# Attention on one core: value matmuls dealt out one by one between score pairs, in step with ScalarE's tiles

## The chip, the cores and the metric

The kernel runs on one core of a Trainium2 chip. The metric is the device time of one execution in microseconds (us).

## The reference

Multi-query attention: 8 batches, 1024 positions, 16 heads of 64, and one key and one value head for each batch.

```python
q = q.transpose(0, 2, 1, 3)
k = k[:, None, :, :]
v = v[:, None, :, :]
scores = np.matmul(q, k.transpose(0, 1, 3, 2)) / np.sqrt(head_dim)
weights = np.exp(scores - np.max(scores, axis=-1, keepdims=True))
weights = weights / np.sum(weights, axis=-1, keepdims=True)
attn_out = np.matmul(weights, v)
return attn_out.transpose(0, 2, 1, 3)
```

Inputs and output are float32. The kernel computes in float16 with float32 sums and leaves out the maximum; a flag at the end sends unfit inputs to a general path, which does not run here.

## The kernel before

The work is cut into 1024 **steps**. Step u makes one **tile**: the scores of 128 keys against 512 queries of two heads (128 x 1024). A pair of heads has two chunks of 512 queries, and a chunk has eight key tiles (`NKT = 8`), so eight steps in a row make one set.

- `scores` (L241): two matmuls (L247), one for each head, into a PSUM tile `sc`. The pool has three such buffers, used in turn, so tile u can be written when tile u-3 has been read.
- Each tile is turned into weights by one engine. Every fifth step from 8 to 1005 (`to_vector`, `VE_EVERY = 5`) goes to VectorE: `vector_exp` reads `sc` once (L211), and four more operations (L217, L227, L235, L237) make three float16 planes `we` out of it. They wait in a list, `pend`, of which `step` takes two for each step. All other tiles go to ScalarE: one ACTIVATE (L260) into `wt`.
- `values` (L307): the products with the values come in **groups**: 128 queries of one head, over the eight tiles of a set, one matmul for a ScalarE tile and three for a VectorE tile (L318). Sets have one or two VectorE tiles, so a group has 10 or 12 matmuls. A set has eight groups, numbered like the steps. Seven groups share one PSUM bank `ot` of two; when a bank is full it is put into `late`, and `inverse` (L263) and `finish` (L272) on VectorE divide by the sums (the 65th column) and store.
- TensorE, VectorE and ScalarE run their instructions in the order in which this program gives them (`manual_schedule`). The main loop takes two steps at a time (`BATCH = 2`): both score tiles, the operations out of `pend`, then value groups that lie `LAG = 18` steps back, then loads of what comes later (`after`):

```python
for _ in range(2 * BATCH):
    if u0 < HURRY:
        ready = nxt < u0 + BATCH - LAG
    else:
        ready = nxt < STEPS - GRP and nxt // GRP * NKT + NKT + 4 <= u0
    if ready:
        pa, ra = divmod(nxt, PSTEPS)
        values(pa, *divmod(ra, NKT))
        nxt += 1
```

So two whole groups (20 or 24 matmuls) follow each pair of score tiles, and from step `HURRY = 1012` on up to four. `last_values` (L331) makes the last set's eight groups tile by tile into two banks `otl` (L344) behind the loop.

Of the kernel before, what the change touches and what calls it, by code (L numbers as in the profile page):

```python
# [28 lines left out]
def attention_main(ctx, tc, q, k, v, out, flag):  # L29
# [14 lines left out]
    NKT = S // P  # L44
    QCH = 512
    NCH = S // QCH
    HP = H // 2
    NP = B * HP
    NQB = QCH // P
    GRP = 2 * NQB  # L50
    NG = NP * NCH * GRP
    GB = 7
# [25 lines left out]
    kv = {}  # L78
    q16 = {}
    qt = {}  # L80
    wt = {}
    osb = {}
    ot = {}
    pend = []
    product = []
    late = []
# [48 lines left out]
    def bank(name):  # L135
        return op.tile([P, 512], FP32, tag="ot", name=name)
# [104 lines left out]
    def scores(p, c, j, by_vector):  # L241
        b = p // HP
        sc = scp.tile([P, 2, QCH], FP32, tag="sc", name=f"sc{p}_{c}_{j}")
        k2t = kv[b]["k2t"]
        for hh in range(2):
            r = 64 * hh
            nc.tensor.matmul(  # L247
                sc[:, hh, :],
                k2t[r : r + 64, j * P : (j + 1) * P],
                qt[b][r : r + 64, p % HP, c * QCH : (c + 1) * QCH],  # L250
                start=True,
                stop=True,
                tile_position=(r, 0),
            )
        if by_vector:
            vector_exp(sc, p, c, j)
            return
        w = wtp.tile([P, 2, QCH], FP16, tag="wt", name=f"wt{p}_{c}_{j}")
        wt[(p, c, j)] = [(w, 0)]
        nc.scalar.activation(out=w, in_=sc, func=EXP, scale=escale, bias=math.log(CS))  # L260

    def inverse(o, g0, n):
        nc.vector.reciprocal(out=rec_all[:, g0 : g0 + n], in_=o[:, 0:n, D])  # L263

    def finish(o, g0, n):

        rec = rec_all[:, g0 : g0 + n]
        i0 = g0 % (OCH * GRP)
        if i0 == 0:
            osb[0] = osbp.tile([P, OCH * GRP, D], FP32, tag="osb", name=f"osb{g0}")  # L270
        ob = osb[0]
        nc.vector.tensor_tensor(  # L272
            out=ob[:, i0 : i0 + n, :],
            in0=o[:, 0:n, 0:D],
            in1=rec.unsqueeze(2).broadcast_to([P, n, D]),
            op=ALU.mult,
        )
        while stored[0] < g0 + n:
            e = stored[0]
            e += GRP // 2 if e >= NG - GRP else GRP  # L280
            if e > g0 + n:
                break
            store(ob, stored[0], e)
            stored[0] = e
        per = HP * NCH * GRP
        if g0 + n == NG:
            check(g0 - GRP // 2, NG, ok_all[:, B:])
        elif checked[0] < B and g0 + n >= min((checked[0] + 1) * per, NG - GRP):
            e = min((checked[0] + 1) * per, NG - GRP)
            b = checked[0]  # L290
            check(b * per, e, None, ok_all[:, b : b + 1])
            checked[0] += 1

    def store(ob, g0, g1):
        p, c = divmod(g0 // GRP, NCH)
        b, hp = divmod(p, HP)
        q0 = c * QCH + g0 % GRP // 2 * P
        j0 = g0 % (OCH * GRP)
        n = g1 - g0
        nc.sync.dma_start(  # L300
            out=out[b, q0 : q0 + n // 2 * P, 2 * hp : 2 * hp + 2, :].rearrange(
                "(qb p) h d -> p qb (h d)", p=P
            ),
            in_=ob[:, j0 : j0 + n, :].rearrange("p (qb h) d -> p qb (h d)", h=2),
        )

    def values(p, c, g):  # L307

        b = p // HP
        qb, hh = divmod(g, 2)  # L310
        gg = (p * NCH + c) * GRP + g
        if gg % GB == 0:
            ot[0] = bank(f"ot{gg}")[:, 0 : GB * 72].rearrange("p (g f) -> p g f", f=72)
        o = ot[0]
        vp = kv[b]["vp"]
        terms = [(j, w, i) for j in range(NKT) for w, i in wt[(p, c, j)]]
        for n, (j, w, i) in enumerate(terms):
            nc.tensor.matmul(  # L318
                o[:, gg % GB, 0 : D + 1],
                w[:, hh, qb * P : (qb + 1) * P],  # L320
                vp[:, i, j, 0 : D + 1],
                start=(n == 0),
                stop=(n == len(terms) - 1),
            )
        if gg % GB == GB - 1 or gg == NG - GRP - 1:
            late.append((o, gg - gg % GB, gg % GB + 1))
        if g == GRP - 1:
            for j in range(NKT):
                del wt[(p, c, j)]

    def last_values():  # L331

# [23 lines left out]
    def check(g0, g1, each, all_=None):  # L356
        n = g1 - g0
        rec = rec_all[:, g0:g1]
        ge = chkp.tile([P, n], FP32, tag=f"ge{n}", name=f"ge{g0}")
        nc.vector.tensor_scalar(  # L360
            out=ge, in0=rec, scalar1=1.0 / SUM_HI, scalar2=None, op0=ALU.is_ge
        )
        both = each
        if both is None:
            both = chkp.tile([P, n], FP32, tag=f"both{n}", name=f"both{g0}")
        nc.vector.scalar_tensor_tensor(  # L366
            out=both, in0=rec, scalar=1.0 / SUM_LO, in1=ge, op0=ALU.is_le, op1=ALU.mult
        )
        if all_ is not None:
            nc.vector.tensor_reduce(out=all_, in_=both, axis=AX.X, op=ALU.min)  # L370

    LAG = 2 * NKT + 2
    STEPS = NP * NCH * NKT
    PSTEPS = NCH * NKT
    BATCH = 2
    LAST_VE = (STEPS - 2 * NKT) // VE_EVERY * VE_EVERY
    HURRY = STEPS - NKT - 4

    def to_vector(u):
        return u % VE_EVERY == 0 and NKT <= u <= LAST_VE  # L380

    def step(u):
        p, r = divmod(u, PSTEPS)
        c, j = divmod(r, NKT)
        scores(p, c, j, to_vector(u))
        for _ in range(2):
            if pend:
                pend.pop(0)()
        if product and u >= LAST_VE + 2 and not pend:
            product.pop()()  # L390

    def after(u):
        p, r = divmod(u, PSTEPS)
# [24 lines left out]
    with tc.manual_schedule():  # L418
        load_kv(0)
        load_q_first(0)  # L420
        make_identity(nc, ident)
        for p in range(1, NFIRST):
            load_q_first(p)
        load_v(0)
        for c in range(NKT):
            load_q(0, c)
        for t in vps:
            for i, ci in enumerate((1.0, C0, C3)):
                nc.gpsimd.memset(t[:, i, :, D : D + 1], ci)
        nc.vector.tensor_copy(out=ident16, in_=ident)  # L430
        nc.vector.memset(ones, 1.0)
        kps = bank("kps0").bitcast(FP16)
        turned[0] = bank("qps0").bitcast(FP16)
        lo, hi = range(NKT // 2), range(NKT // 2, NKT)
        q0 = q16[("first", 0)]
        nc.scalar.copy(out=q0[:, 0 : NKT // 2, :], in_=qf[:, 0 : NKT // 2, :])  # L436
        first_k(kps, 0)
        first_q(turned[0], 0, lo)
        first_q_out(turned[0], 0, lo, nc.scalar.copy)
        first_k_out(kps, 0)  # L440
        first_k(kps, 1)
        first_k_out(kps, 1)
        nc.vector.tensor_copy(out=q0[:, NKT // 2 :, :], in_=qf[:, NKT // 2 :, :])
        prep_v(0)
        for c in range(NKT):
            turn_q(0, c)
        nxt = 0
        for u0 in range(0, STEPS, BATCH):
            us = range(u0, u0 + BATCH)
            for u in us:  # L450
                step(u)
            for f in late:
                pend.insert(0, lambda f=f: inverse(*f))
                pend.insert(min(2, len(pend)), lambda f=f: finish(*f))
            del late[:]
            for _ in range(2 * BATCH):
                if u0 < HURRY:
                    ready = nxt < u0 + BATCH - LAG
                else:
                    ready = nxt < STEPS - GRP and nxt // GRP * NKT + NKT + 4 <= u0  # L460
                if ready:
                    pa, ra = divmod(nxt, PSTEPS)
                    values(pa, *divmod(ra, NKT))
                    nxt += 1
            for u in us:
                after(u)
        assert nxt == STEPS - GRP
        assert not product
        for f in pend:
            f()  # L470
        for f in late:
            inverse(*f)
            finish(*f)
        last_values()
        okm = chkp.tile([P, 1], FP32, tag="okm", name="okm")
        nc.vector.tensor_reduce(out=okm, in_=ok_all, axis=AX.X, op=ALU.min)
        cnt = bank("cnt")[0:1, 0:1]
        nc.tensor.matmul(cnt, okm, ones, start=True, stop=True)
        nc.vector.tensor_scalar(
            out=flag, in0=cnt, scalar1=P - 0.5, scalar2=None, op0=ALU.is_lt  # L480
        )
# [120 lines left out]
```

## Time and profile before

| | |
|---|---|
| median of 3 runs | 782.24 us (781.58 to 783.35) |
| profiled execution | 783.46 us, span 781.5 us |
| ScalarE (ACT) busy | 98% |
| TensorE (PE) busy | 93% |
| VectorE (DVE) busy | 93% |
| GpSimd (POOL) busy | 8% |

A line of the profile names the engine, the line of the kernel (L260), the operation, output<-input, how often, the busy time, and the idle time before it with the engine that ended it. In the timeline the columns are the start in us, the length in us, engine, line, operation and count, and in brackets how long the engine had been idle and what it waited for. In the table by windows, each engine's busy time is followed by its count in brackets, then the granted TensorE clock, the DMA share and GB/s. PE is the matmuls, PEld the weight loads; the matmul lengths overlap.

### The profile page before, as it was taken

What the parts mean: (1) busy time and instruction counts of PE and PEld (TensorE: products, weight loads), DVE (VectorE), ACT (ScalarE), POOL (GpSimd) and SP (SyncE); (2) the same over time, 40 slices, a digit from 0 to 9 for tenths busy, and PEclk for the clock granted to TensorE, in tenths of its full rate; (3) what the DMA queues carried; (4) which work ended last, traced back from release to release, by engine and by line L of the source; (5) the groups of instructions that cost most, each with busy time, mean ns of one, the idle gap of its engine ahead of it and who ended that gap; (6) DMA issues with size and microseconds to landing.
All of it is one profiled execution on the core that took longest, in us unless ns stands there. A gap on an engine that the chain in (4) does not pass through costs nothing.

```text
span 781.5 us, 30669 instructions
## 1 busy us (share of the span) xinstructions
PE 728.7 (93%) x13474; PEld 474.1 (61%) x13474; DVE 728.9 (93%) x1349; ACT 762.5 (98%) x827; POOL 65.9 (8%) x99
## 2 busy tenths in 40 slices
PE   5999999999999999999999999999999999999996
PEld 2566666656666666666656666666666666666665
DVE  3899999999999999999999999999999999999992
ACT  7999999999999999999999999999999999999996
POOL 4210002100011002010020100201002100000000
PEclk8899999999999999999999999999999999999999
DMA  9949118582193813756155552556417373111113
GB/s 169 146 93 164 55 44 157 97 136 57 29 170 76 154 33 76 150 103 115 45 91 123 124 95 56 90 128 115 101 42 125 89 149 71 51 35 55 43 43 84
DMA packets 168633, 73.84 MB, mean 94 GB/s; under 512 B 93744, under 2 KB 161328, under 8 KB 168496
## 3 DMA queue, kind: packets, MB, share of 16 engines
q1 hardware_dynamic: 148864, 53.76, 32.5%
q0 software_dynamic: 18576, 17.57, 14.8%
q8 instruction: 106, 1.74, 1.0%
q10 hardware_dynamic: 1056, 0.52, 0.3%
q14 instruction: 31, 0.25, 0.1%
HBM read 37.75 MB, written 33.55 MB: 91 GB/s over the span
## 4 chain that ended last, share of the span: by engine, by line
ACT 38%; DVE 21%; PE 21%; issue 19%; DMA 1%; DVEq 0%; ACTq 0%
ACT wt L260 38%; PE ot L318 11%; PE sc L247 9%; DVE we L211 8%; DVE osb L272 3%; DVE we L237 3%; DVE mm L235 3%; DVE m L217 2%; DVE we L227 2%; DVE rec_all L263 1%; DMA qf<-in_q_dram 1%; PE otl L344 0%; DVE both L366 0%; DVE ok_all L370 0%; DVE ge L360 0%
## 5 line engine op out<-in xcount | busy, mean ns | idle before, releaser
L260 ACT ACTIVATE wt<-sc 128x1024 f16<-128x1024 f32 x824 | 760.0, 1062 | 7.4 <-PE sc L247 6.1
L318 PE MATMUL ot<-vp,wt 128*128 128x65 f16 x6528 | 418.4, 194 | 0.6 <-issue 0.6
L318 PEld LDWEIGHTS <-wt 128*128 128x128 f16 x6528 | 325.8, 98 | 114.8 <-issue 114.8
L247 PE MATMUL sc<-qt,k2t 64*128 64x512 f16 x2048 | 352.8, 386 | 41.2 <-ACT wt L260 29.1
L318 PE MATMUL ot<-vp,we 128*128 128x65 f16 x4800 | 352.2, 193 | 0.0
L318 PEld LDWEIGHTS <-we 128*128 128x128 f16 x4800 | 250.0, 97 | 30.6 <-issue 30.6
L211 DVE TENSOR_SCALAR we<-sc 128x1024 int16<-128x1024 f32 x200 | 243.6, 1218 | 23.2 <-PE sc L247 22.1
L247 PEld LDWEIGHTS <-k2t 64*128 64x128 f16 x2048 | 93.2, 94 | 149.0 <-issue 111.0
L237 DVE TENSOR_TENSOR we<-we,mm 128x1024 f16<-128x1024 f16 x200 | 136.9, 685 | 0.0
L235 DVE TENSOR_TENSOR mm<-m 128x1024 f16<-128x1024 f16 x200 | 136.5, 683 | 0.0
L272 DVE TENSOR_TENSOR osb<-ot,rec_all 128x448 f32<-128x448 f32 x146 | 90.5, 620 | 4.2 <-DVE rec_all L263 0.2
L217 DVE TENSOR_SCALAR m<-we 128x1024 int16<-128x1024 int16 x200 | 85.8, 429 | 0.0
L227 DVE TENSOR_SCALAR we<-we 128x1024 int16<-128x1024 int16 x200 | 83.5, 418 | 0.0
L104 POOL DMA_DIRECT2D vp<-in_v_dram x8 | 7.5, 936 | 388.5 <-PE ot L318 388.4
L121 POOL DMA_DIRECT2D q<-in_q_dram x64 | 35.0, 571 | 26.7 <-DMA qt<-q 22.9
L263 DVE RECIPROCAL rec_all<-ot 128x7 f32<-128x7 f32 x146 | 28.6, 196 | 8.7 <-PE ot L318 8.6
L190 POOL TENSOR_SCALAR k16d<-knat 128x512 f16<-128x512 f32 x14 | 21.4, 1537 | 134.7 <-DMA knat<-in_k_dram 134.7
L202 DVE TENSOR_SCALAR vp<-vp 128x512 f16<-128x512 f16 x16 | 3.9, 286 | 2.0 <-DMA vp<-in_v_dram 2.0
L155 PE MATMUL kps<-ident,k 128*64 128x128 f16 x16 | 1.3, 314 | 4.5 <-DVE k L146 4.5
L184 DVE COPY qt<-qps 128x512 f16<-128x512 f16 (+1 forms) x2 | 1.1, 554 | 3.3 <-PE qps L171 3.3
L155 PEld LDWEIGHTS <-k 128*64 128x64 f16 x16 | 0.8, 159 | 4.7 <-DVE k L146 4.7
L436 ACT ACT_TABLE_LOAD x1 | 1.3, 1283 | 1.9 <-issue 1.9
(29 smaller groups left out, 22.2 us busy)
## 6 DMA issues: line engine op xcount, KB each, us to landing
out_dram<-osb SPq DMA_DIRECT2D x127, 256.0 KB, 2.4
q<-in_q_dram POOLq DMA_DIRECT2D x56, 256.0 KB, 8.8
knat<-in_k_dram SPq DMA_DIRECT2D x7, 256.0 KB, 4.1
q<-in_q_dram POOLq DMA_DIRECT2D x8, 192.0 KB, 8.0
vp<-in_v_dram POOLq DMA_DIRECT2D x8, 128.0 KB, 4.4
qt<-q SPq DMA_TRANSPOSE x64, 3.9
qf<-in_q_dram ACTq DMA_DIRECT2D x2, 256.0 KB, 4.4
knat<-in_k_dram SPq DMA_DIRECT2D x2, 128.0 KB, 3.8
```

The source lines that it names most:

```text
L121: nc.gpsimd.dma_start(out=q16[(b, c)], in_=q[b, c * P : (c + 1) * P, h0:, :].rearrange("p h d -> p (h d)"),)
L190: nc.gpsimd.tensor_scalar(out=k16d[:, :, i, :], in0=st["knat"], scalar1=kscale, scalar2=None, op0=ALU.mult)
L211: nc.vector.tensor_scalar(out=t, in0=sc, scalar1=15.0 * 1024, scalar2=0.0, op0=ALU.add, op1=ALU.max)
L217: lambda: nc.vector.tensor_scalar(out=m.bitcast(I16), in0=t, scalar1=0x3FF, scalar2=0x3C00, op0=ALU.bitwise_and, op1=ALU.bitwise_or,)
L227: lambda: nc.vector.tensor_scalar(out=w3[:, 0].bitcast(I16), in0=t, scalar1=0x7C00, scalar2=None, op0=ALU.bitwise_and,)
L235: pend.append(lambda: nc.vector.tensor_tensor(out=m2, in0=m, in1=m, op=ALU.mult))
L237: lambda: nc.vector.tensor_tensor(out=w3[:, 2], in0=w3[:, 1], in1=m2, op=ALU.mult)
L247: nc.tensor.matmul(sc[:, hh, :], k2t[r : r + 64, j * P : (j + 1) * P], qt[b][r : r + 64, p % HP, c * QCH : (c + 1) * QCH], start=True, sto ...
L260: nc.scalar.activation(out=w, in_=sc, func=EXP, scale=escale, bias=math.log(CS))
L263: nc.vector.reciprocal(out=rec_all[:, g0 : g0 + n], in_=o[:, 0:n, D])
L272: nc.vector.tensor_tensor(out=ob[:, i0 : i0 + n, :], in0=o[:, 0:n, 0:D], in1=rec.unsqueeze(2).broadcast_to([P, n, D]), op=ALU.mult,)
L318: nc.tensor.matmul(o[:, gg % GB, 0 : D + 1], w[:, hh, qb * P : (qb + 1) * P], vp[:, i, j, 0 : D + 1], start=(n == 0), stop=(n == len(terms ...
```

## The change

The value matmuls are no longer given out in whole groups. `values` now returns a list of single matmuls, and `plan` works out in advance how many of them shall have been given out by the end of each pair of steps. It reckons that a tile of ScalarE stands for a constant number of matmul times (`each`), that the two score tiles of a pair use up `OTHER = 21` of them, and it pulls the sum by an eighth of the difference towards the number that lies one group ahead of the former order. Values may lie up to two groups further ahead than before (`AHEAD = 2`). From step 1010 on (`HURRY`, before 1012) whole groups follow again, up to four for each pair of steps, and a set's groups may come two steps earlier than before. When a bank is full, the operations `inverse` and `finish` are put at the head of `pend` with one other operation between them; when two are full at once, they follow each other.

```diff
-    def values(p, c, g):
-        b = p // HP
+    def values(gg):
+        p, c = divmod(gg // GRP, NCH)
+        g = gg % GRP
...
         terms = [(j, w, i) for j in range(NKT) for w, i in wt[(p, c, j)]]
-        for n, (j, w, i) in enumerate(terms):
+
+        def one(n, j, w, i):
+            last = n == len(terms) - 1
             nc.tensor.matmul(
                 o[:, gg % GB, 0 : D + 1],
                 w[:, hh, qb * P : (qb + 1) * P],
                 vp[:, i, j, 0 : D + 1],
                 start=(n == 0),
-                stop=(n == len(terms) - 1),
+                stop=last,
             )
...
+        return [lambda n=n, t=t: one(n, *t) for n, t in enumerate(terms)]
...
+    OTHER = 21
+    AHEAD = 2
-    HURRY = STEPS - NKT - 4
+    HURRY = STEPS - NKT - 6
...
+    def plan():
+        at = range(LAG, HURRY, BATCH)
+        tiles = [sum(not to_vector(u) for u in range(u0, u0 + BATCH)) for u0 in at]
+        upto = [0]
+        for g in range(HURRY - LAG + AHEAD):
+            many = sum(to_vector(g // GRP * NKT + j) for j in range(NKT))
+            upto.append(upto[-1] + NKT + 2 * many)
+        each = (upto[HURRY - LAG] + OTHER * len(tiles)) / sum(tiles)
+        due, done = {}, 0.0
+        for u0, n in zip(at, tiles):
+            done += each * n - OTHER
+            done += (upto[u0 + BATCH - LAG + 1] - done) / 8
+            due[u0] = round(done)
+        return due
...
-        nxt = 0
+        nxt = made = 0
+        todo = []
+        due = plan()
         for u0 in range(0, STEPS, BATCH):
             us = range(u0, u0 + BATCH)
             for u in us:
                 step(u)
+            new = []
             for f in late:
-                pend.insert(0, lambda f=f: inverse(*f))
-                pend.insert(min(2, len(pend)), lambda f=f: finish(*f))
+                new += [lambda f=f: inverse(*f), lambda f=f: finish(*f)]
+            if len(new) == 2:
+                new[1:1] = pend[:1]
+                del pend[:1]
+            pend[:0] = new
             del late[:]
-            for _ in range(2 * BATCH):
-                if u0 < HURRY:
-                    ready = nxt < u0 + BATCH - LAG
-                else:
-                    ready = nxt < STEPS - GRP and nxt // GRP * NKT + NKT + 4 <= u0
-                if ready:
-                    pa, ra = divmod(nxt, PSTEPS)
-                    values(pa, *divmod(ra, NKT))
-                    nxt += 1
+            if u0 < HURRY:
+                while made < due.get(u0, 0):
+                    if not todo:
+                        if nxt >= u0 + BATCH + AHEAD - LAG:
+                            break
+                        todo = values(nxt)
+                        nxt += 1
+                    todo.pop(0)()
+                    made += 1
+            else:
+                for _ in range(2 * BATCH):
+                    if not todo and nxt < STEPS - GRP and nxt // GRP * NKT + NKT + 2 <= u0:
+                        todo = values(nxt)
+                        nxt += 1
+                    for f in todo:
+                        f()
+                    todo = []
             for u in us:
                 after(u)
```

More of the change, by code (lines that the diff above doesn't have):

```diff
@@ L305, in store @@
         )
-    def values(p, c, g):
-        b = p // HP
+    def values(gg):
+        p, c = divmod(gg // GRP, NCH)
+        g = gg % GRP
         qb, hh = divmod(g, 2)
-        gg = (p * NCH + c) * GRP + g
         if gg % GB == 0:
@@ L314, in values @@
         o = ot[0]
-        vp = kv[b]["vp"]
+        vp = kv[p // HP]["vp"]
         terms = [(j, w, i) for j in range(NKT) for w, i in wt[(p, c, j)]]
-        for n, (j, w, i) in enumerate(terms):
+        def one(n, j, w, i):
+            last = n == len(terms) - 1
             nc.tensor.matmul(
@@ L322, in values @@
                 start=(n == 0),
-                stop=(n == len(terms) - 1),
+                stop=last,
             )
[L325 to L329, printed above, removed]
+            if not last:
+                return
+            if gg % GB == GB - 1 or gg == NG - GRP - 1:
+                late.append((o, gg - gg % GB, gg % GB + 1))
+            if g == GRP - 1:
+                for x in range(NKT):
+                    del wt[(p, c, x)]
+        return [lambda n=n, t=t: one(n, *t) for n, t in enumerate(terms)]
     def last_values():
```

## The prediction

> **What bounds the kernel now.** I read the page's engine shares and chain first, then the waits over the whole span, then the timeline of single tiles. A tile is one 128x1024 block of scores (two matmuls of L247); I number tiles 0 to 1023 in their order, and name places by the last digit, because every tenth pair of steps has the same mix: digits 0 and 5 go to VectorE (L211, "V0", "V5"), the other eight to ScalarE (L260, "A1" to "A9"). S4 is the score of tile 4.
>
> ```profile
> span 781.5 us, 30669 instructions
> PE 728.7 (93%) x13474; PEld 474.1 (61%) x13474; DVE 728.9 (93%) x1349; ACT 762.5 (98%) x827; POOL 65.9 (8%) x99
> PEclk8899999999999999999999999999999999999999
> ACT 38%; DVE 21%; PE 21%; issue 19%; DMA 1%; DVEq 0%; ACTq 0%
> L260 ACT ACTIVATE wt<-sc 128x1024 f16<-128x1024 f32 x824 | 760.0, 1062 | 7.4 <-PE sc L247 6.1
> ...
> PE sc L247 <- ACT wt L260: 29.1, 96, 0.5
> DVE we L211 <- PE sc L247: 22.1, 45, 1.3
> PE sc L247 <- DVE we L211: 7.6, 19, 0.9
> ACT wt L260 <- PE sc L247: 6.1, 19, 0.7
> ```
>
> ScalarE is 98% busy, but the chain runs through three engines, so they wait on each other. The granted clock is full but for the first slices, so a stretch of matmuls keeps its length. The waits (total, times, longest) say how: TensorE's scores stand still for a buffer that ScalarE still reads, 96 times, about once for each ten tiles, while ScalarE waits visibly only 19 times. There are three score buffers, so S7 can't be written before A4 is done. That wait sits at one place:
>
> ```profile
> 436.49 1.09 ACT L260 ACTIVATE wt<-sc 128x1024 f16<-128x1024 f32 x1
> 437.39 1.11 ACT L260 ACTIVATE wt<-sc 128x1024 f16<-128x1024 f32 x1
> 437.63 0.39 PE L247 MATMUL sc<-qt,k2t 64*128 64x512 f16 x2 [0.37 <-ACT wt L260]
> 438.29 1.12 ACT L260 ACTIVATE wt<-sc 128x1024 f16<-128x1024 f32 x1
> 438.69 0.39 PE L247 MATMUL sc<-qt,k2t 64*128 64x512 f16 x2
> 439.20 1.13 ACT L260 ACTIVATE wt<-sc 128x1024 f16<-128x1024 f32 x1
> ...
> 437.62:438.68 1.06, 0.72 (x20) 0.67 (x20) 1.00 0.53 147
> ```
>
> These are tiles 574 to 578. A574 starts at 436.49, ends at 437.58, S577 starts at 437.63 (1.14 after A574's start), then 20 value matmuls (the row by window, x20), then S578 at 438.69, and A578 at 439.20, which is 0.51 behind its score. ScalarE's pace is 0.90 a tile (436.49, 437.39, 438.29, 439.20), and the least distance from a score's start to its activation is 0.49 (next rows), so with 20 values this place has 0.02 us to spare.
>
> ```profile
> 411.17 1.22 DVE L211 TENSOR_SCALAR we<-sc 128x1024 int16<-128x1024 f32 x1
> 412.44 0.39 PE L247 MATMUL sc<-qt,k2t 64*128 64x512 f16 x2 [0.83 <-DVE we L211]
> 413.61 0.39 PE L247 MATMUL sc<-qt,k2t 64*128 64x512 f16 x2
> 413.83 0.38 PE L247 MATMUL sc<-qt,k2t 64*128 64x512 f16 x2
> 414.10 1.02 ACT L260 ACTIVATE wt<-sc 128x1024 f16<-128x1024 f32 x1
> 415.48 1.02 ACT L260 ACTIVATE wt<-sc 128x1024 f16<-128x1024 f32 x1 [0.36 <-PE sc L247]
> ...
> 412.44:413.60 1.16, 0.84 (x24) 0.79 (x24) 1.00 1.16 217
> ...
> 440.07 0.39 PE L247 MATMUL sc<-qt,k2t 64*128 64x512 f16 x2
> 440.50 1.22 DVE L211 TENSOR_SCALAR we<-sc 128x1024 int16<-128x1024 f32 x1 [0.35 <-PE sc L247]
> ```
>
> Here are the other links: V540 starts at 411.17 and S543, which takes its buffer, at 412.44 (1.27). S543 to S544 takes 1.17 with 24 values between; S544 to S545 0.22; S544 to A544 0.49; S580 to V580 0.43. The row at 415.48 is A546, a digit 6: it comes 1.38 behind A544 instead of 0.90, since 24 values stood between S545 and S546. That is the loss the change goes for: after a pair with a V tile ScalarE has one tile less to live on.
>
> **The change part by part.** Instruction counts of all engines and queues stay as they are; the value matmuls are only dealt out differently between the score pairs, and their LDWEIGHTS with them. The plan's arithmetic: 11088 value matmuls over 496 pairs and 794 ScalarE tiles give (11088 + 21 x 496) / 794 = 27.08 a tile, so a pair with two ScalarE tiles is followed by 2 x 27.08 - 21 = 33, one with a V tile by 6, moved by an eighth of the lead. Over ten steps that comes out as 7 to 9 behind pair (0,1), 32 or 33 behind (2,3), 7 or 8 behind (4,5), 33 or 34 behind (6,7) and 29 to 32 behind (8,9); before, each had 20 or 24.
>
> What a longer stretch costs is in the trace, near the end:
>
> ```profile
> 769.28 0.60 PE L247 MATMUL sc<-qt,k2t 64*128 64x512 f16 x4
> 769.81 1.19 PE L318 MATMUL ot<-vp,wt 128*128 128x65 f16 x32
> 770.93 0.75 PE L247 MATMUL sc<-qt,k2t 64*128 64x512 f16 x4
> ...
> 769.50:770.92 1.42, 1.11 (x32) 1.06 (x32) 1.00 0.00 0
> ```
>
> 32 values make 1.65 from pair to pair, 1.43 from the second score on; one value is (1.06 - 0.10)/31 = 0.031 of weight loading. From the 24-value row the second score to the next pair is 1.17 + 0.031 x (n - 24): 1.46 for 33.3, 1.39 for 31, 1.43 for 32.5.
>
> Now the path that sets the end. S7 still waits for A4, whatever stood before it: three buffers, in turn. From A4's start: S7 +1.14, S8 +1.46, so S8 is at 2.60 and A8 could start at 3.09. But between A4 and A8 ScalarE has only A6 and A7 (5 is VectorE's): it is ready at 3 x 0.90 = 2.71. A8 is 0.38 late, where now it is on time. The lateness is handed on: S9 +0.22, S10 behind 31 values +1.39, V10 +0.43 (VectorE idle, as at 440.50), S13 into V10's buffer +1.27, S14 behind 32.5 values +1.43, A14 +0.49. A4 to A14:
>
> 1.14 + 1.46 + 0.22 + 1.39 + 0.43 + 1.27 + 1.43 + 0.49 = 7.83 us for ten tiles.
>
> Each step is a fixed precedence (buffer, TensorE's order, data), so ten tiles can't be faster than that. Now they take two L211 intervals:
>
> ```profile
> L211 DVE TENSOR_SCALAR we<-sc 128x1024 int16<-128x1024 f32 x183 | 222.9, 1218 | 17.6 <-PE sc L247 16.5
> ```
>
> 183 of them lie in the window from 60 to 740 us, 680/183 x 2 = 7.43. The same loop with 22.4 values in each stretch (1.12 each) is 6.91, below 7.43, so it doesn't bind today. The difference is +0.40 us, times 99 tens from step 18 to 1008: +39.6. The gain at digits 2 and 6 (S2 and S6 come behind 7 or 8 values) is inside that comparison: there TensorE will stand waiting for A9's and A3's buffers instead. Bounds for the loop: a value by the 20 and 24 rows alone, (1.17 - 1.06)/4 = 0.0275, gives 1.43, 1.36 and 1.40, sum 7.74; the 32-value row with 0.031 on it gives 1.47, 1.40, 1.45, sum 7.87. I take the middle row, which is nearest in kind (stretches with we tiles).
>
> VectorE: 728.9 us busy over 102 tens is 7.1 each, hidden under 7.83 with 0.7 to spare. The changed order in pend only matters when two inverse and finish pairs come together, which 34 values (four group ends at most, where a bank closes at every seventh) can't make: nothing. Values run up to two groups ahead: a first value then needs tile u0-8 at step u0; the product of a V tile is issued at u0-3, whose buffer S(u0) itself waits for: nothing, at most 0.1 a ten if it shows. Output stores (SP) and loads (POOL) keep their steps: nothing, by the chain's 1% DMA.
>
> The end:
>
> ```profile
> 7.35 17.55 ACT L260 ACTIVATE wt<-sc 128x1024 f16<-128x1024 f32 x19 [0.70 <-PE sc L247]
> ...
> 767.32 6.67 ACT L260 ACTIVATE wt<-sc 128x1024 f16<-128x1024 f32 x7
> 772.96 0.62 DVE L272 TENSOR_TENSOR osb<-ot,rec_all 128x448 f32<-128x448 f32 x1 [0.17 <-DVE rec_all L263]
> 773.64 2.33 PE L344 MATMUL otl<-vp,wt 128*128 128x65 f16 x64 [0.84 <-DVE osb L272]
> 775.89 0.18 DVE L263 RECIPROCAL rec_all<-otl 128x4 f32<-128x4 f32 x1 [1.21 <-PE otl L344]
> ```
>
> ScalarE ends at 773.99, but L344 starts at 773.64 because the finish at 772.96 frees its bank, and its end releases 775.89. Hurrying two steps earlier puts the last 32 values behind pair 1020 and none behind 1022: the finish moves up by about 1.6 (770.93 against 769.28), L344 is then left with the eight matmuls of the last tile after 773.99, 0.4 with their latency: -1.5. If the bank still comes late, 0. The 40 to 48 values that two groups a step bring stand behind pairs whose four tiles are all ScalarE's: 1.14 + 1.17 + 24 x 0.031 + 0.49 = 3.54 against 4 x 0.90: nothing.
>
> Sum: +39.6 - 1.5 = +38 on the profiled execution's 783.46; on the median of the runs, 782.24 (the profiled one is 1.2 above it), 820.
>
> **Weighed against the skill.** ScalarE's 0.90 enters the 2.71. The Trainium skill, ScalarE: Activation LUTs, section What ACT_TABLE_LOAD costs, gives 186 ns + 0.833 N with immediate operands and an overlap of 93, an estimate of 0.946 a tile here. By it eight tiles would need 7.57, more than the 7.43 measured, so the trace disagrees and decides; the loop of 7.83 would be the same by both, as it only passes A4 and A14, and the first rival's 7.59 would be 7.82.
>
> **The rivals.**
> One: only ScalarE's leg counts. If the V10 leg were shorter than its rows (A14 not delayed again), A8's lateness alone remains: 1.14 + 1.46 + 0.49 + 5 x 0.90 = 7.59, +0.16 a ten, +15.8 - 1.5: 797. For it: VectorE often starts late now for its own queue's sake. Against it: each of its links is a row above. Chance 0.12.
>
> Two: worse. VectorE's inverse and finish or a check fall in front of V10 and join the loop; +0.2 a ten would be about 0.6 for a third of the tens, +20: 840. Against it: the 0.7 to spare. Chance 0.06.
>
> Three, the other side: S8 is not held. ScalarE's visible waits close and nothing takes their place: -6.1 and -1.5 of the end, 775 (all of ScalarE's distance to its pace, the 766.6 from 7.35 to 773.99 less 824 x 0.90 = 742, would be 25, and 757). It decides at 21 values behind (6,7): up to there S8 starts by 2.71 - 0.49 = 2.22 after A4; 33 are dealt. It could hold if S7's release came 0.38 earlier than in the row at 437.63. Chance 0.07. The Trainium skill's Perfetto Trace Analysis, section Optimization Strategy, says to take the most-contended engine, find its gaps and make what ends them start sooner; by that rule, which looks at the 98% engine alone, this rival would be the forecast, and the 96 waits for a buffer are what it leaves out.
>
> Four: gain at 2 and 6 and loss at 8 cancel, 782. Against it: the loop is a sum, not a balance. Chance 0.03.
>
> **How the numbers follow.** My forecast has 0.72, with 808 to 832 as its own range (7.71 to 7.95 a ten: the loop's bounds of 7.74 and 7.87, with 0.03 less and 0.08 more for the length of an activation, which the rows show at 1.02 to 1.13). With rival one the range is 796 to 832 and leaves out 0.16. A measurement of this kernel tells about 0.2% (1.6 us) from no change: slower 0.90 (forecast and rivals one and two), same 0.03, faster 0.07.
>
> **What would show it.** In the changed kernel: L211 every 3.9 us in the mean instead of 3.7; S7's wait for ScalarE longer than now, and S8 starting directly behind some 33 values, with ScalarE idle about 0.25 in front of A8 and a little in front of A14; ScalarE's visible wait for scores from 6.1 to over 20 us in total; visible waits at digits 2 and 6 gone; VectorE waiting for S0. L344 ending within 0.5 of ScalarE's end. I am wrong if S8 starts within 2.22 of A4, if V10 doesn't start 0.43 behind S10, or if TensorE is found at a value matmul ahead of a waiting score.

## The result, and the profile after

The changed kernel takes 821.29 us (median of five runs, 820.98 to 821.70) against 782.24: ratio 1.0497, 95% interval 1.0483 to 1.0512. It is 39 us slower; the forecast was 820.

The page and the waits of the changed kernel (total us, times, longest us):

```profile
span 819.2 us, 30668 instructions
PE 727.7 (89%) x13474; PEld 461.0 (56%) x13474; DVE 731.1 (89%) x1349; ACT 779.3 (95%) x827; POOL 66.9 (8%) x99
L260 ACT ACTIVATE wt<-sc 128x1024 f16<-128x1024 f32 x824 | 776.8, 1029 | 29.8 <-PE sc L247 21.8
...
DVE we L211 <- PE sc L247: 59.9, 93, 2.3
PE sc L247 <- DVE we L211: 43.2, 98, 0.9
PE sc L247 <- ACT wt L260: 32.8, 106, 0.5
ACT wt L260 <- PE sc L247: 21.8, 96, 1.3
PE ot L321 <- DVE osb L272: 4.3, 10, 1.3
```

Every engine does the same work with less of its time: TensorE went from 93% to 89%, VectorE from 93% to 89%, ScalarE from 98% to 95%. No engine became the bound; they wait for each other in turn. TensorE waits for VectorE's buffer 98 times (19 before) and ScalarE for scores 96 times (19 before): about once for each ten tiles, as a closed path of ten tiles would have it.

One turn of it in the timeline (start, length, engine, operation, idle time before it and its releaser):

```profile
434.65 0.61 PE L247 MATMUL sc<-qt,k2t 64*128 64x512 f16 x4
435.15 1.02 ACT L260 ACTIVATE wt<-sc 128x1024 f16<-128x1024 f32 x1 [0.39 <-PE sc L247]
435.51 0.39 PE L247 MATMUL sc<-qt,k2t 64*128 64x512 f16 x2
436.22 0.39 PE L247 MATMUL sc<-qt,k2t 64*128 64x512 f16 x2 [0.32 <-ACT wt L260]
437.69 0.61 PE L247 MATMUL sc<-qt,k2t 64*128 64x512 f16 x4
438.18 5.80 ACT L260 ACTIVATE wt<-sc 128x1024 f16<-128x1024 f32 x6 [0.18 <-PE sc L247]
439.31 0.61 PE L247 MATMUL sc<-qt,k2t 64*128 64x512 f16 x4
439.75 1.23 DVE L211 TENSOR_SCALAR we<-sc 128x1024 int16<-128x1024 f32 x1 [0.74 <-PE sc L247]
440.20 0.39 PE L247 MATMUL sc<-qt,k2t 64*128 64x512 f16 x2
441.02 0.39 PE L247 MATMUL sc<-qt,k2t 64*128 64x512 f16 x2 [0.43 <-DVE we L211]
442.47 0.60 PE L247 MATMUL sc<-qt,k2t 64*128 64x512 f16 x4
...
436.50:437.69 1.19, 1.15 (x34) 1.09 (x34) 1.00 1.07 229
```

Read it from S4 (434.65): A4 at 435.15 (ScalarE had been idle 0.39); S7 at 436.22, when A4's buffer is free (1.07); then 34 values (the row by window) and S8 at 437.69 (1.47); A8 at 438.18, idle before it, 3.03 behind A4 where its pace would give 2.71; pair (0,1) at 439.31 (1.62 from pair to pair); V10 at 439.75, VectorE idle 0.74 before it; S13 at 441.02, released by V10 (1.27); S14 at 442.47 (1.45). S4 to S14 is 7.82. Over the whole span, by the first and last L211 of each kernel, before and after (count; shortest, median and longest in ns; first and last start):

```profile
L211 DVE TENSOR_SCALAR we<-sc x200: 1209/1216/1225, 15.5 to 756.7; 128x1024 int16<-128x1024 f32 x100
...
L211 DVE TENSOR_SCALAR we<-sc x200: 1209/1224/1225, 15.4 to 796.0; 128x1024 int16<-128x1024 f32 x100
```

(796.0 - 15.4)/199 x 2 = 7.84 us for ten tiles; before, 7.45. That is +0.39 in each of 99 tens. The end got shorter:

```profile
810.29 2.90 ACT L260 ACTIVATE wt<-sc 128x1024 f16<-128x1024 f32 x3
...
811.23 2.43 PE L351 MATMUL otl<-vp,wt 128*128 128x65 f16 x64 [0.30 <-DVE osb L272]
```

ScalarE ends at 813.19, the span at 819.2: 6.0, against 7.5 before (773.99 and 781.5).

### The profile page after: what moved, and what is told of

Its sections match the earlier page's. It is cut to its first block, busy times and chain, and to the rows that moved or that the text cites. A ratio compares the mean times of both kernels' runs of the same rounds, so it can differ in the third digit from the quotient of the medians.

```text
span 819.2 us, 30668 instructions
## 1 busy us (share of the span) xinstructions
PE 727.7 (89%) x13474; PEld 461.0 (56%) x13474; DVE 731.1 (89%) x1349; ACT 779.3 (95%) x827; POOL 66.9 (8%) x99
## 3 DMA queue, kind: packets, MB, share of 16 engines
q8 instruction: 106, 1.74, 0.9%
## 4 chain that ended last, share of the span: by engine, by line
PE 35%; ACT 34%; DVE 17%; issue 12%; DMA 1%; ACTq 0%; DVEq 0%; SPq 0%
ACT wt L260 34%; PE ot L321 21%; PE sc L247 13%; DVE we L211 8%; DVE osb L272 2%; DVE we L237 2%; DVE mm L235 2%; DVE m L217 1%; DVE we L227 1%; DVE rec_all L263 0%; DMA qf<-in_q_dram 0%; DMA knat<-in_k_dram 0%; PE otl L351 0%; ACTq L260 0%; DVE vp L202 0%
## 5 line engine op out<-in xcount | busy, mean ns | idle before, releaser
L260 ACT ACTIVATE wt<-sc 128x1024 f16<-128x1024 f32 x824 | 776.8, 1029 | 29.8 <-PE sc L247 21.8
L247 PE MATMUL sc<-qt,k2t 64*128 64x512 f16 x2048 | 349.2, 386 | 76.7 <-DVE we L211 43.2
L321 PE MATMUL ot<-vp,we 128*128 128x65 f16 x4800 | 358.1, 193 | 0.3 <-DVE osb L272 0.3
L211 DVE TENSOR_SCALAR we<-sc 128x1024 int16<-128x1024 f32 x200 | 244.0, 1220 | 60.5 <-PE sc L247 59.9
L321 PEld LDWEIGHTS <-we 128*128 128x128 f16 x4800 | 254.6, 97 | 60.8 <-issue 60.7
L247 PEld LDWEIGHTS <-k2t 64*128 64x128 f16 x2048 | 79.1, 94 | 166.3 <-issue 138.4
L272 DVE TENSOR_TENSOR osb<-ot,rec_all 128x448 f32<-128x448 f32 x146 | 90.4, 619 | 3.7 <-DVE rec_all L263 0.2
(29 smaller groups left out, 22.4 us busy)
```

The costliest lines, as they stand in the source:

```text
L211: nc.vector.tensor_scalar(out=t, in0=sc, scalar1=15.0 * 1024, scalar2=0.0, op0=ALU.add, op1=ALU.max)
L247: nc.tensor.matmul(sc[:, hh, :], k2t[r : r + 64, j * P : (j + 1) * P], qt[b][r : r + 64, p % HP, c * QCH : (c + 1) * QCH], start=True, sto ...
L272: nc.vector.tensor_tensor(out=ob[:, i0 : i0 + n, :], in0=o[:, 0:n, 0:D], in1=rec.unsqueeze(2).broadcast_to([P, n, D]), op=ALU.mult,)
L321: nc.tensor.matmul(o[:, gg % GB, 0 : D + 1], w[:, hh, qb * P : (qb + 1) * P], vp[:, i, j, 0 : D + 1], start=(n == 0), stop=last,)
```

## The experiments

The digits and names (A4, S7, V10) are those of the prediction. All ratios are to the kernel before, run beside. In the traces a tile's lateness is the distance from the activation before it, less ScalarE's pace of 0.903; means and medians are over steps 40 to 1000.

### Two halves of the loop against ScalarE's leg alone

Rival one had only A8's lateness count. Moving values from behind (6,7) to behind (8,9) takes that lateness away and leaves the loop's sum as it is:

```diff
-            done += each * n - OTHER
+            done += each * n - OTHER + {6: -13, 8: 13}.get(u0 % 10, 0)
```

> The changed kernel with 13 value matmuls moved from behind the pair with digit 6 to behind the pair with digit 8 (about 21 and 42 instead of 33 and 31; the sum behind digits 2, 6 and 8 is 95.7 instead of 96.7). Theory, the ten-tile loop A4, S7, S8, S9, S10, V10, S13, S14, A14: it passes all three long stretches, so only their sum counts; -1.0 x 0.031 x 99 = -3: 816 to 821 us, and A8 on time all the same. Rival, only A8's lateness behind 33 values costs time: the mean 0.29 in front of A8 is gone, 99 x 0.29 = 28 less: about 793.

Measured: 822.54 us, ratio 1.0513 (1.0496 to 1.0531). A8's mean lateness fell from 0.29 to 0.01, and A1's rose from 0.03 to 0.28: the lateness moved to the next place of the loop and the time stayed. The rival's 793 is out. The time is 1.5 us above the range that the loop gave. TensorE waited 10.0 us for banks in this run (4.3 in the changed kernel), and 3.75 of it, against 0.73, between S13 and S14, so on the loop: that takes up the 3 us that the smaller sum should have saved.

The sum itself was changed by one number, `OTHER = 10`:

> The changed kernel with OTHER = 10 instead of 21: about 30 values behind digits 2, 6 and 8 and 10 to 12 behind 0 and 4; the sum of the three is 89.7 instead of 96.7. Loop theory: 7.0 x 0.031 x 99 = 21 less: 798 to 802. Rival, A8's lateness alone: 3 values fewer behind digit 6, 0.09 x 99 = 9 less: 812.

Measured: 802.98 us, 1.0264 (1.0246 to 1.0281). One us above the loop's range and nine below the price of A8 alone: 18 us less than the change, where the sum gives 21 and A8 alone 9.

### The link through V10, and a confounded pair

To lengthen one link I gave VectorE a second operation behind L211, for one digit only:

```diff
+        if (c * NKT + j + p * NCH * NKT) % 10 == 0:   # 5 in the other run
+            nc.vector.tensor_scalar(out=t[:, :, 0:128], in0=sc[:, :, 0:128],
+                scalar1=15.0 * 1024, scalar2=0.0, op0=ALU.add, op1=ALU.max)
```

> The changed kernel with a second operation on VectorE behind L211 for tiles of digit 0 only: it does a quarter of the tile (128x256) again, with the same result, about 0.33 us (a quarter of L211's 1.07 beyond its fixed part, and 0.06). The score buffer is held that much longer. Loop theory: V10 to S13 is a link of the loop, all of it counts, 100 x 0.33 = +33: 848 to 858. Rival, the loop's second half is not on the path (A8's lateness alone sets the time): S13 has the time to wait, at most +10: 821 to 831. Rival, VectorE's total work: +33 here and in the run with digit 5 alike.

> The same second operation, for tiles of digit 5 only. V5's buffer is needed by S8, which in the changed kernel stands behind 33 values and starts 2.53 after A4, while V5 ends about 1.8 after A4: with 0.33 more still before it. Loop theory: V5 is no link of the loop; 0 to +5: 821 to 826. Rival, VectorE's total work is the bound: +33, 854, as with digit 0.

Measured: 839.59 (1.0726, 1.0709 to 1.0744) and 837.61 (1.0701, 1.0684 to 1.0719). Neither came as expected. The waits of the first told why:

```profile
PE sc L256 <- ACT wt L269: 82.1, 203, 0.5
...
PE sc L256 <- DVE we L211: 1.6, 6, 0.4
```

TensorE hardly waited for VectorE any more (6 times), and twice per ten tiles for ScalarE. The three score buffers aren't handed out strictly in turn: they are chosen when the program is built, and with V0's buffer held longer S3 had been given A1's and S4 V0's; in the other run S8 had A6's and S9 V5's (so the compiled programs place them). The trace agrees: in the first run S3 starts 0.05 behind A1's end and 0.33 before the second operation on V0 ends, in the median. The link that I meant to lengthen was gone: V10 to S13 was 1.33 in the mean instead of 1.28. In the changed kernel itself the turn is kept but for four scores (S158, S288, S668 and S798 start 0.05 to 0.16 before the tile three back has been read), so forcing it there would change little. With a tag for each buffer the turn is forced:

```diff
-        sc = scp.tile([P, 2, QCH], FP32, tag="sc", name=f"sc{p}_{c}_{j}")
+        u = (p * NCH + c) * NKT + j
+        sc = scp.tile([P, 2, QCH], FP32, tag=f"sc{u % 3}", name=f"sc{p}_{c}_{j}")
...
-    scp = ctx.enter_context(tc.tile_pool(name="scp", bufs=3, space=PSUM))
+    scp = ctx.enter_context(tc.tile_pool(name="scp", bufs=1, space=PSUM))
```

> The run with a second operation on VectorE for tiles of digit 0 (839.6), but with the three score buffers used strictly in turn (a tag for each). In that run S3 had been given A1's buffer instead of V0's, so the link V10 to S13 wasn't there to be lengthened. Now it is: S13 waits for the second operation, whose end lies 1.68 behind V10's start (1.26 to its start and 0.42) instead of 1.22, so the link is 1.73 instead of 1.27. Loop theory: 99 x 0.46 = +46: 862 to 870. Rival, the link isn't on the path: about 838 as in that run.

Measured: 866.14 (one round, 1.1061, 1.1040 to 1.1082). The same instructions as in the run with 839.59, 27 us apart by the buffers' turn alone. The link in the timeline, and the waits:

```profile
446.74 1.22 DVE L211 TENSOR_SCALAR we<-sc 128x1024 int16<-128x1024 f32 x1 [0.87 <-PE sc L257]
448.00 0.42 DVE L215 TENSOR_SCALAR we<-sc 128x256 int16<-128x256 f32 x1
448.48 0.39 PE L257 MATMUL sc<-qt,k2t 64*128 64x512 f16 x2 [0.92 <-DVE we L215]
...
PE sc L257 <- DVE we L215: 89.5, 99, 1.3
```

V10 to S13 is 1.74 instead of 1.27, 99 times. +0.47 a ten is +46 us on 821, and 866 - 821 = 45 was measured: this link counts in full, so V10 lies on the path. VectorE has the same work in the run with 839.59, so it isn't its work that costs the 45. (The second operation took 0.42 us, where 0.33 had been reckoned.)

The run with V5 cost 16 us where 0 to 5 were expected. Link by link, in the mean, its trace (an execution of 839.5 us) has 0.18 a ten more than the changed kernel, all of it at three links. S9 to S10 is 0.11 longer: of the 11.0 us that TensorE waited for a bank's finish (below; 4.3 before) 10.3 stand there, 1.4 in the changed kernel. V0 started 0.05 later behind its score. S8 to S9 is 0.03 longer, and S9 now has V5's buffer. So VectorE's 0.7 to spare isn't there at every place, and with the buffers changed this run says nothing on V5 alone.

```profile
PE ot L330 <- DVE osb L281: 11.0, 29, 1.0
```

### The end alone

```diff
-    HURRY = STEPS - NKT - 4
+    HURRY = STEPS - NKT - 6
...
-                    ready = nxt < STEPS - GRP and nxt // GRP * NKT + NKT + 4 <= u0
+                    ready = nxt < STEPS - GRP and nxt // GRP * NKT + NKT + 2 <= u0
```

> The kernel before with the change's second part alone: two groups per step from step 1010 on instead of 1012, a set's groups two steps earlier. Theory: the finish of the last full bank no longer holds the last products (L344) behind ScalarE's end: -1.5, 780.7 us. Rival: the end isn't on the path, 0: 782.4. Worse: 40 to 48 values earlier hold a score, +0.3.

Measured: 782.02, 0.9997 (0.9981 to 1.0012): nothing that this can tell. Two banks come full at once there, and the order of `pend` before finishes them in reverse (the new order in the change prevents that; in this run the last stores carry data that are not theirs). So once more with the changed kernel's order of the finishes:

> The kernel before in its whole groups with the end of the changed kernel and its order of the finishes (in the run with the end alone the last two banks were finished in reverse order, so the last stores were wrong, and the last products still waited for a bank). Theory: from ScalarE's end to the end of the span 6.0 as in the changed kernel, against 7.5 before: -1.0 to -1.5, 781.0. Rival: nothing, 782.4.

Measured: 781.15, 0.9985 (0.9972 to 0.9999). The end's gain is 1.2 us, interval 0.1 to 2.2; the prediction had 1.5. In the trace the span ends 6.0 behind ScalarE, as in the changed kernel.

### Looking for a better deal

If only the sum behind 2, 6 and 8 counted, values should go behind 0 and 4:

```diff
-            done += each * n - OTHER
+            done += SHARE[u0 % 10]   # {0: 16, 2: 29, 4: 17, 6: 20, 8: 29.8}
```

> The changed kernel with the values dealt out by a fixed share for each digit: about 16 behind pair (0,1), 28.5 behind (2,3), 17.5 behind (4,5), 20.5 behind (6,7) and 29 behind (8,9). The loop's three stretches sum to 78 instead of 96.7: 7.84 - 18.4 x 0.031 = 7.27 us for ten tiles, A8 on time (20.5 values are under 21), A2 and A6 on time too (16 and 17.5). ScalarE's own pace is 8 x 0.903 = 7.22 and VectorE's work 7.1. Loop theory: 7.27 to 7.36 a ten against 7.44 before, and 1.5 at the end: 765 to 774 us, faster than both kernels. Rival, VectorE binds (its inverse and finish and the checks have no room under 7.4): 778 to 782. Rival, dealing out single values costs by itself (groups broken up between score pairs): above 790.

> The same with flatter shares: 20, 25, 20, 20 and 26.5 behind the pairs with digits 0, 2, 4, 6 and 8: the sum of the loop's stretches is 71.7. Loop theory: not bound by the loop (7.07); A2 and A6 have one value to spare instead of five, so every late VectorE tile shows there: between the kernel before and the run with 16 and 17.5, 770 to 779. If it is as fast as that run, the room behind digits 0 and 4 isn't what counts.

Measured: 793.48 (1.0134, 1.0118 to 1.0149), and with {0: 20, 2: 25, 4: 20, 6: 20, 8: 26.8} 789.15 (1.0073, 1.0058 to 1.0088). Both better than the change (821), as the loop says, and both worse than the kernel before, which it doesn't.

793.48, the first of the two, is also what the rival said that single values cost something by themselves (above 790). The trace speaks against it: S13 to S14 with 28.5 single values takes 1.32 in the median, where the price of whole groups gives 1.17 + 4.5 x 0.031 = 1.31.

The forecast missed two things. The first is a longer path through the same links: from A4 it runs on from S14 to S15, past the values behind (4,5), to S16 and A16. With the first share that is 1.14 + 1.06 + 0.22 + 1.33 + 0.43 + 1.27 + 1.31 + 0.22 + 0.97 + 0.49 = 8.44, where ScalarE's pace for nine tiles is 8.13. The path spans two tiles of digit 6, A6 and A16, so the 0.31 over comes to 0.15 for each on average; in the trace a digit 6 is 0.25 late in the mean. The flat share gives 8.31, so 0.09 for each; measured 0.22. The kernel before, with 22.4 in each stretch, gives 8.25, so 0.06; measured 0.11. So the path gives the right order and about half of the size: in the traces A4 to A16 is 8.71, 8.64 and 8.46 in the mean. No run lengthened this path alone, so it is argued and not shown.

If it holds, four of the five stretches lie on it, and the fifth, behind (0,1), can't take more than about 21 (as the prediction has it for (6,7)), so an even deal would be near the best that whole stretches allow.

The second is a wait which the kernel before doesn't have:

```profile
PE ot L321 <- DVE osb L272: 7.4, 18, 1.5
```

This is the first share. Values that run a group ahead reach a bank before VectorE has finished it. Of the 7.4 us 6.4 stand behind (4,5), so on the longer path; with the flat share it is 6.5 of 7.0.

So I left the groups whole and used a place where TensorE stands still anyway, in front of S7:

```diff
+            first = todo[: BETWEEN.get(u0 % 10, 0)]   # {6: 7}, or {6: 12}
             step(u0)
+            for f in first:
+                f()
             step(u0 + 1)
```

> The kernel before in its whole groups, with the end of the changed kernel, and one thing else: at digit 6 seven of the 20 or 24 value matmuls stand between S6 and S7, where TensorE waits for A4's buffer (the wait in front of S7 is 0.65 in the median of the kernel before, of which 0.22 is the two scores' own distance; 7 values take 0.32 + 6 x 0.031 + 0.13 = 0.63). They cost nothing there, and S8, S9 and S10 come 7 x 0.031 = 0.22 earlier. Theory: TensorE's scores are late at digits 2 and 6 (0.16 a ten together) because it stands still at S7 and can't make it up; 0.22 more of room takes most of that: -10 to -16 and -1 at the end: 766 to 772. Rival, VectorE binds at 7.4: 778 to 782. Rival, breaking the pair costs 0.22 that isn't hidden: 790 or more.

> The same with 12 values between S6 and S7. They take 0.79, so S7 starts 0.15 later than A4 allows, and S8 is no earlier than with 7. Theory: no better than with 7, 0 to +8 on it. If it is faster, A4's end isn't what S7 waits for.

Measured: 779.02 with seven (0.9961, 0.9942 to 0.9979) and 779.44 with twelve (0.9950, 0.9933 to 0.9968): the two don't differ. Both beat the kernel before by 0.4 to 0.5%, 1.2 us of it by the end, so the place itself is worth about 2 us. S8 stood 2.05 behind A4 in the median instead of 2.26, the 0.22 as worked out, but A6's lateness fell only from 0.11 to 0.10, which the sum over twelve tiles doesn't give either (8.25 - 0.22 is below 8.13). Some of the room went into the next wait: S1, which needs A8's buffer, stood 0.43 behind S0 in the median instead of 0.32. The expectation of 766 to 772 fell.

What was left looked like the limit of 21 values behind S5 and S1. With these seven values in place, the last run moved four from behind (4,5) to behind S7 and four from behind (0,1) to behind (8,9):

> The kernel with seven values between S6 and S7 (779.0), and eight values moved: four from behind pair (4,5) to behind S7, where A8 has 0.24 us of room, and four from behind pair (0,1) to behind pair (8,9). In that run A6 was 0.10 late in the mean and A2 0.04, since 20 or 24 values behind S5 and S1 are more than the 21 that fit between the buffer of A2 (A8) and A6 (A2). With 16 or 20 they fit. Theory, ScalarE's late starts behind values are what is left: up to 0.13 a ten, 99 x 0.13 = 13, half of it given back by V tiles that come later: 768 to 774. Rival, VectorE's queue binds at 7.4 a ten whatever TensorE does: 777 to 780, with the lateness moved to other digits.

Measured: 782.16, 0.9993 (0.9984 to 1.0002). It lost what the seven had won. By the path above the eight moved values make its three stretches behind 6, 8 and 2 longer by eight and the one behind 4 shorter by four, 0.12 more in all, which puts its sum back over 8.13, to 8.15. That was worked out afterwards and not tried apart, and since the sum runs below the traces, the cause stays open.

## Why the prediction was right

- **The place.** S7 waits for A4, 33 values follow, A8 is late: forecast 0.38, mean 0.29 in the changed kernel. A4 to S7 came out at 1.07 in the turn shown (1.09 in the mean) instead of 1.14, as activations were shorter (1.029 in the mean against 1.062).
- **The loop.** 7.83 forecast, 7.84 measured, and each link is in the rows: 1.07, 1.47, 1.62 (0.22 and 1.40), 0.44, 1.27, 1.45 and 0.50, sum 7.82. That it is the loop and not A8 alone was shown by the moved values (822.5), its slope by `OTHER = 10` (803.0), and its second half by the forced turn (866.1). That the sum hits to 0.01 is partly luck: in the mean the first link is 0.05 shorter than forecast, and S9 to S10, S10 to V10 and S13 to S14 together 0.05 longer.
- **The gain that was given back.** A2 and A6 were 0.05 and 0.11 late before and 0.01 and 0.04 after: that part did what it promises, 0.1 a ten, under a loss of 0.5 at A4 and A8.
- **The end.** -1.5 forecast; -1.5 in the traces (7.5 to 6.0 behind ScalarE's end) and -1.2, with an interval of -0.1 to -2.2, in the timing of that part.
- **Small misses.** "Nothing" for the values that run ahead was not quite right: TensorE waited 4.3 us in ten places for a bank's finish. Not for a V tile's product, which I had looked at, but for `finish` (L272, which reads the bank into `osb`), which I hadn't. S7's wait grew only a little (32.8 us in all 106 waits for ScalarE, against 29.1 in 96). And TensorE was not found standing in front of S2 and S6 for the buffers of A9 and A3, as the prediction has it (idle below 0.01 in the mean); it stood in front of S13, as 43.2 us, 7.6 before.
- **Rivals.** VectorE's queue did not join (840 forecast for that): VectorE waited 59.9 us for scores. The rule of the most-contended engine (the Trainium skill, Perfetto Trace Analysis, section Optimization Strategy) would have promised a gain here. The trace disagrees: the gaps of the 98% engine were closed at digits 2 and 6, 0.1 a ten, and 0.5 a ten opened at 4 and 8.
- **Where the same reasoning fell short.** The loop over ten tiles was enough for this change, but not to design a better one. A path over twelve tiles, found only after both shares had failed, gives about half of the lateness that they and the kernel before show at digit 6; waits for a bank on that path are a further part, and the rest is open.

## What to carry to other kernels

When three engines are each over 90% busy and hand each other a few buffers, look for a closed path: start to start through a buffer's release, an in-order stretch, the data, the next release. Here its sum against the present period said what a reordering costs before anything was built. It did not say what a better order would gain: longer paths and the waits for other buffers have to be summed too. Work placed behind an instruction that waits for a buffer starts only when that buffer is free, however much work its consumer still has; an instruction that must stand still anyway is the place to put work in front of (worth about 2 us here).

## What was not expected

- ScalarE's activations of the same 128x1024 tile took 1.062 us in the mean before and 1.029 after, where TensorE stood still more often; the pace stayed 0.90. The cause wasn't tried.
- A pool of three buffers didn't mean the third tile back: one operation of 0.42 us more on a tile changed which buffer the next ones got, and with the turn forced the same instructions took 866.1 instead of 839.6.
- The price of a value matmul, 0.031, held in stretches of 7 to 45; breaking a pair of scores open for seven of them showed no loss where S7 had stood 0.65 behind S6 before.
